# Recurrent mixers regrouped on TensorE, and masks added by one fp32r product for all heads of a bank

## The chip, the cores and the metric

The kernel runs on one core of one Trainium2 chip. The metric is device time in microseconds (us) of one execution. Before the change the median of three runs is 1646.14 us (1645.08 to 1652.29).

## What is computed

Two layers of a hybrid mixer over 1024 tokens of width 1024, each followed by a residual sum and a layer norm. A layer projects its input to some 4000 columns, feeds four groups of four heads of 64, and projects their outputs back:

```python
y_a = flat(banded_attention(q_a, k_a, heads(cols['a_v']), A_WINDOW, a_sinks)) * silu(cols['a_z'])
...
h_b = mlstm_chunkwise(...)
y_b = jax.nn.sigmoid(cols['b_o']) * flat(h_b) * silu(cols['b_z'])
...
o_c = hgrn2_chunkwise(heads(silu(cols['c_q'])), heads(jnp.log(f_c)), heads(1.0 - f_c), heads(cols['c_i']))
...
o_d = nsa_attention(...)
y = jnp.concatenate([y_a, y_b, y_c, y_d], axis=-1)
```

Group A is attention in a window of 128 tokens, with a sink. Group D joins three attentions: over compressed blocks, over selected blocks, and in a window of 512. Groups B and C are recurrences in chunks: a state is carried from chunk to chunk, and inside a chunk every query meets the earlier keys with a decay. In B the weight of key s for query t is

```python
D = jnp.where(causal, b[..., :, None] - b[..., None, :] + i_[..., None, :], -jnp.inf)
...
S = jnp.einsum('bhtd,bhsd->bhts', q_, k_) * jnp.exp(D - m_t[..., None])
num = jnp.einsum('bhts,bhsv->bhtv', S, v_) + w_inter[..., None] * jnp.einsum('bhtk,bhvk->bhtv', q_, C)
```

and in C the output of a chunk is the sum of the products inside it and of the queries with the state S:

```python
o = jnp.einsum('bhts,bhsv->bhtv', A, v_) + jnp.einsum('bhtk,bhkv->bhtv', q_ * jnp.exp(a), S)
S_new = jnp.exp(a_last[:, :, 0, :])[..., None] * S + jnp.einsum('bhsk,bhsv->bhkv', k_ * jnp.exp(a_last - a), v_)
```

All operands and results are float32.

## The kernel before

Tokens go in tiles of 128. A *stage* is one half (512 tokens, four tiles) of one layer, so there are four stages; each works through the groups D, C, A, B in this order. Projections and the attention scores take each float32 operand as a high and a low fp32r part and add three products (hi x hi, hi x lo, lo x hi; the weights are split by `load_piece`, L260 on, with ACT for the high and POOL for the low part). Products of plain float32 operands, such as P V and most of B and C, run as two records each in the trace; a transpose is one.

The order of work comes from two places. At the bottom of `tile_hybrid` a loop weaves groups: for each of the four tiles of the current group's mixer it issues one projection of the next group (`projections`, L1136, and the loop below it). Over that the framework's scheduler puts each engine's instructions in order when the program is built, by a simulated timeline; it also sets the semaphores. On the chip every engine then runs its own queue in that order. PSUM has one bank each per buffer: three for scores (psS), two for transposes (psT), two for projections (pj), one for outputs (psO).

The places that the change touches:

- **Constants** (L93 to L130, L221 to L245). `masks` holds three 128x128 masks of 0 and -1e30 (causal, its complement for the window's far edge, and the transposed causal one for B); `cmask` masks the compressed keys; `identb` is a bf16 identity. A mask is added to scores in PSUM by a product of the identity with the mask. `sel` is 128x512 of ones in rows 32c+h, so that four rows of it spread one row of numbers over 128 partitions. `load_consts` brings them in through buffers of tag P, with a cast on POOL (L242), in the first stage after the first projection.
- **`scores`** (L354 to L418), used by A and D. The keys are cut into at most two pieces of up to 512; a PSUM bank holds `hb` heads (four of 128 keys, two of 256, one of more). For each head there are two fp32r products (L377, and L381 or L379) and then bf16 mask products of 128 columns: L383 for the window's far edge, L385 for the diagonal. DVE then takes the maximum of the bank (L387), ACT the exponential (L392).
- **`group_D` front**, L620: the compressed mask is added for four heads by one bf16 product.
- **`group_C`**, the loop over chunks. `front(c+1)` comes first (decays on POOL, L761 to L764; products S_ab, L796 and L801, of 64x64). Then, for four heads, the state product L831 (64 rows, 64 columns, only if there is an earlier chunk) and the product with Vc L832 (128 rows, 64 columns) alternate into one bank Oc. Then the transposes kt_ps (L836), their copy kh on ACT (L838), the products of the new state s_ps (L843) and its update on DVE (L847 to L849).
- **`group_B`**, preparation (L962 to L999) once a stage: gates `lf`, transposed to rows `r_ps`, running sums and maxima `R` (rB, rU, rM, rE, each 128x128, where chunk c and head h sit in row 32c+h), and the carry `rk` by chunk. `front(c)` (L1002 on) fills two banks SW: the causal mask by a bf16 product of 256 columns (L1008), the row rM spread over 128 partitions by a plain float32 product of four rows for each head (L1012), and beside them Q K (L1017). `xb` (L1032) spreads rE in the same way, 64 partitions to a head.

Of the kernel before, what the change touches and what calls it, by code (L numbers as in the profile page):

```python
# [89 lines left out]
def consts():  # L90
# [5 lines left out]
    c['masks'] = np.stack([lo, up, lo.T], 1).astype(np.float32)  # L96
# [29 lines left out]
    sel = np.zeros((128, 4, 128), np.float32)  # L126
    for h in range(4):
        sel[h::32, h, :] = 1.0
    c['sel'] = sel.reshape(128, 512)
# [16 lines left out]
def tile_hybrid(ctx, tc, I, out, dbg=None, depth=DEPTH):  # L146
# [3 lines left out]
    def f(ap):  # L150
        return ap.bitcast(F32)
# [69 lines left out]
    masks = const.tile([128, 3, 128], BF16, name="masks_bf")  # L221
    cmask = const.tile([128, NT, 64], BF16, name="cmask_bf")
    identb = const.tile([128, 128], BF16, name="ident_bf")
# [4 lines left out]
    sel = const.tile([128, 512], F32, name="sel_sb")  # L228
# [4 lines left out]
    G.tensor_copy(identb, ident)  # L233

    def load_consts():

        for name, dst in (('masks', masks), ('cmask', cmask), ('lvm', lvm)):
            d2 = dst.rearrange("p a b -> p (a b)")
            n = d2.shape[1]
            m_ = mp.tile([128, 512], F32, tag="P", name="m_", bufs=PB)  # L240
            SY.dma_start(m_[:, :n], I[name] if name == 'lvm' else I[name].rearrange("p a b -> p (a b)"))
            G.tensor_copy(d2, m_[:, :n])  # L242
        for name, dst in (('rowok', rowok), ('rope_e', rope_e), ('impk', impk), ('sel', sel)):
            SY.dma_start(dst, I[name])
# [109 lines left out]
    def scores(i, k0, A1, A2, kcols, Kblk, weigh, win, sink=None, A3=None):  # L354
# [10 lines left out]
        for c, (a, b) in enumerate(cuts):  # L365
            n = b - a
            hb = 4 if n <= 128 else 2 if n <= 256 else 1
            Pc = [mp.tile([128, 2, 512], F32, tag="P", name="P", bufs=PB) for _ in range(2)]
            P.append(Pc)
            for h0 in range(0, NH, hb):  # L370
                Sp = psS.tile([128, 512], F32, tag="S", name="S_ps")[:, :hb * n].rearrange("p (h k) -> p h k", h=hb)
                for z in range(hb):
                    h = h0 + z
                    o_ = Sp[:, z, :]
                    m0, m1 = lo_mask and c == 0, b == nk * 128
                    kc_ = kcols(h, a, b)
                    PE.matmul(o_, A1[:, h, :], kc_, start=True, stop=False)  # L377
                    if Kblk is not None:
                        PE.matmul(o_, A3[:, h, :], Kblk[:, a:b], start=False, stop=not (m0 or m1))  # L379
                    else:  # L380
                        PE.matmul(o_, A2[:, h, :], kc_, start=False, stop=not (m0 or m1))  # L381
                    if m0:
                        PE.matmul(o_[:, 0:128], identb, masks[:, 1, :], start=False, stop=not m1)  # L383
                    if m1:
                        PE.matmul(o_[:, n - 128:n], identb, masks[:, 0, :], start=False, stop=True)  # L385
# [54 lines left out]
    def groups(stage):  # L440
# [83 lines left out]
        def group_D():  # L524
# [86 lines left out]
            def front(t):  # L611
# [8 lines left out]
                PE.matmul(Sc3, identb, bc(cmask[:, i, :nc_], 4, 0), start=True, stop=False)  # L620
# [76 lines left out]
        def group_C():  # L697
# [121 lines left out]
            for c in range(NTH):  # L819
# [4 lines left out]
                O = psO.tile([128, 256], F32, tag="O", name="Oc")  # L824
                for ct in range(2):
                    for hh in range(2):
                        h = 2 * ct + hh
                        rows = slice(64 * hh, 64 * hh + 64)
                        o_ = O[rows, ct * 128:(ct + 1) * 128]
                        if i > 0:  # L830
                            PE.matmul(o_, St[rows, ct, :], qe[rows, ct * 128:(ct + 1) * 128], start=(ct == 0), stop=False)  # L831
                        PE.matmul(o_, Vc[:, c, 64 * h:64 * h + 64], Af[:, hh, ct, :], start=(i == 0 and ct == 0), stop=(ct == 1))  # L832
                if i < NT - 1:
# [4 lines left out]
                    S.copy(out=kh.rearrange("p a b -> p (a b)"), in_=kt_ps)  # L838
                    s_ps = psT.tile([128, 2, 64], F32, tag="T", name="s_ps")
# [73 lines left out]
        def group_B():  # L913
# [55 lines left out]
            V.tensor_tensor(lf[:, 0, :].rearrange("p (c w) -> p c w", c=4)[:, :, 0:4], l1, l0, op=OP.subtract)  # L969
            V.tensor_copy(lf[:, 1, :].rearrange("p (c w) -> p c w", c=4)[:, :, 0:4], gi[:, :, 12:16])  # L970
# [5 lines left out]
            rk = sm.tile([128, 4], F32, tag="rk", name="rk")  # L976
            V.tensor_tensor_scan(rB, ones, r_ps[:, 0, :], 0.0, op0=OP.mult, op1=OP.add)
# [4 lines left out]
            if hf == 1:  # L982
                V.tensor_copy(rk[0:4, 0:1], mcar[0:4, :])
            for c in range(NTH):
                p_ = slice(32 * c, 32 * c + 4)
                dst = rk[32 * c + 32:32 * c + 36, 0:1] if c < NTH - 1 else mcar[0:4, :]
# [4 lines left out]
            V.tensor_scalar(rE, rM, rk[:, 0:1], None, op0=OP.add)  # L991
            u_ps = psT.tile([128, 2, 128], F32, tag="T", name="u_ps")
# [9 lines left out]
            def front(c):  # L1002
                i = T0 + c
                cs_ = slice(c * 128, (c + 1) * 128)
                p_ = slice(32 * c, 32 * c + 4)
                SW = [psS.tile([128, 512], F32, tag="S", name="SW") for _ in range(2)]
                for hh in range(2):
                    PE.matmul(SW[hh][:, 0:256].rearrange("p (h t) -> p h t", h=2), identb, bc(masks[:, 2, :], 2, 0),  # L1008
                              start=True, stop=False)
                    for ct in range(2):  # L1010
                        h = 2 * ct + hh
                        PE.matmul(SW[hh][:, ct * 128:(ct + 1) * 128], sel[p_, h * 128:(h + 1) * 128], rM[p_, :],  # L1012
                                  start=False, stop=(ct == 1))
# [17 lines left out]
                for p in range(2):  # L1031
# [178 lines left out]
```

## Time and profile before

| | |
|---|---|
| runs, median (range) | 1646.14 us (1645.08 to 1652.29) |
| the profiled execution, its own time | 1654.33 us |
| its span | 1652.5 us |
| mean granted TensorE clock | 0.962 |
| chain that ended last, TensorE and DVE | 66% and 19% |
| moved by DMA | 126.70 MB, mean 77 GB/s |

The span is the time from the first to the last recorded instruction; the execution's own time has a little around it. PE is TensorE's matmuls, PEld its weight loads, DVE VectorE, ACT ScalarE, POOL GpSimd, SP the queue that issues DMAs. A row of the timeline gives the start and the duration in us, the engine, the line, the operation, the tile written and the tiles read, for a matmul rows*columns of the array and the shape that is streamed, and how many records are merged (x4). Durations of matmuls overlap, because they are pipelined: the time that one occupies TensorE is the distance to the next start. A row of a source line or a tile gives the shortest, median and longest duration in ns. Brackets name idle time before an instruction, and who ended it.

### The profile page before, as it was taken

What the parts mean: (1) busy time and instruction counts of PE and PEld (TensorE: products, weight loads), DVE (VectorE), ACT (ScalarE), POOL (GpSimd) and SP (SyncE); (2) the same over time, 40 slices, a digit from 0 to 9 for tenths busy, and PEclk for the clock granted to TensorE, in tenths of its full rate; (3) what the DMA queues carried; (4) which work ended last, traced back from release to release, by engine and by line L of the source; (5) the groups of instructions that cost most, each with busy time, mean ns of one, the idle gap of its engine ahead of it and who ended that gap; (6) DMA issues with size and microseconds to landing.
All of it is one profiled execution on the core that took longest, in us unless ns stands there. A gap on an engine that the chain in (4) does not pass through costs nothing.

```text
span 1652.5 us, 29596 instructions
## 1 busy us (share of the span) xinstructions
PE 1538.6 (93%) x10948; PEld 1206.1 (73%) x10948; DVE 1026.2 (62%) x2454; ACT 798.3 (48%) x1865; POOL 848.7 (51%) x1173
## 2 busy tenths in 40 slices
PE   4999999899979989999998999999997999999995
PEld 3787688678767657787877768786886765688774
DVE  6256835874787776357447676456448777735737
ACT  2356535544356664455435653444434666434541
POOL 4733784546643138634575468544565321873442
PEclk9999999989989999999999999999998999799997
DMA  5322023441441001224134212233134210022311
GB/s 180 91 64 59 15 76 90 155 142 45 120 144 52 26 1 46 65 68 142 44 108 153 74 33 56 55 107 105 36 105 160 55 52 1 20 66 65 90 52 51
DMA packets 64752, 126.70 MB, mean 77 GB/s; under 512 B 10112, under 2 KB 16032, under 8 KB 64608
## 3 DMA queue, kind: packets, MB, share of 16 engines
q1 hardware_dynamic: 63744, 122.72, 25.4%
q8 instruction: 86, 1.41, 0.4%
q10 hardware_dynamic: 864, 2.10, 0.3%
q14 instruction: 58, 0.48, 0.1%
HBM read 114.30 MB, written 10.49 MB: 76 GB/s over the span
## 4 chain that ended last, share of the span: by engine, by line
PE 66%; DVE 19%; POOL 5%; issue 3%; DMA 3%; ACT 3%; SPq 0%; DVEq 0%; POOLq 0%; ACTq 0%
PE ps_f L307 7%; PE ps_f L306 6%; PE ps_f L305 6%; PE ps_p L290 5%; PE ps_p L291 4%; PE ps_p L292 4%; PE ps_pt L427 4%; PE O L434 4%; PE ps_o L478 2%; PE ps_o L476 2%; PE S_ps L377 2%; DVE QK L950 2%; PE ps_o L477 2%; PE S_ab L796 2%; DMA w_raw<-in_w_in 2%
## 5 line engine op out<-in xcount | busy, mean ns | idle before, releaser
L267 POOL TENSOR_TENSOR w_split<-w_raw,w_split 128x512 fp32r<-128x512 f32 (+2 forms) x320 | 416.0, 1307 | 380.7 <-ACT w_split L266 350.6
L266 ACT CAST w_split<-w_raw 128x512 fp32r<-128x512 f32 (+2 forms) x320 | 194.4, 611 | 238.9 <-DMA w_raw<-in_w_in 109.5
L305 PE MATMUL ps_f<-hT_hi,w_split 128*128 128x512 f32 x608 | 246.0, 405 | 0.0
L306 PE MATMUL ps_f<-hT_lo,w_split 128*128 128x512 f32 x608 | 244.0, 401 | 0.0
L307 PE MATMUL ps_f<-hT_hi,w_split 128*128 128x512 f32 x608 | 243.5, 402 | 0.0
L290 PE MATMUL ps_p<-w_split,hT_hi 128*128 128x256 f32 (+1 forms) x768 | 227.3, 298 | 8.0 <-DVE hT_lo L257 5.5
L291 PE MATMUL ps_p<-w_split,hT_hi 128*128 128x256 f32 (+1 forms) x768 | 222.8, 291 | 0.0
L292 PE MATMUL ps_p<-w_split,hT_lo 128*128 128x256 f32 (+1 forms) x768 | 222.1, 290 | 0.0
L392 ACT ACTIVATE P<-S_ps,stt 128x256 f32<-128x256 f32 (+3 forms) x256 | 133.8, 530 | 91.7 <-DVE stt L387 49.7
L290 PEld LDWEIGHTS ps_p<-w_split,hT_hi 128*128 128x128 f32 x768 | 149.4, 195 | 14.1 <-DVE hT_lo L257 7.2
L291 PEld LDWEIGHTS ps_p<-w_split,hT_hi 128*128 128x128 f32 x768 | 149.6, 195 | 2.2 <-issue 1.2
L292 PEld LDWEIGHTS ps_p<-w_split,hT_lo 128*128 128x128 f32 x768 | 149.2, 194 | 1.8 <-issue 1.2
L307 PEld LDWEIGHTS ps_f<-hT_hi,w_split 128*128 128x128 f32 x608 | 115.4, 190 | 28.1 <-issue 2.8
L306 PEld LDWEIGHTS ps_f<-hT_lo,w_split 128*128 128x128 f32 x608 | 115.3, 190 | 26.3 <-issue 3.3
L305 PEld LDWEIGHTS ps_f<-hT_hi,w_split 128*128 128x128 f32 x608 | 115.5, 190 | 25.6 <-issue 1.9
L387 DVE TENSOR_REDUCE stt<-S_ps 128x1 f32<-128x384 f32 (+3 forms) x182 | 111.1, 625 | 28.4 <-PE S_ps L385 15.1
L476 PE MATMUL ps_o<-w_split,Y 128*128 128x512 f32 x256 | 114.7, 448 | 8.6 <-DVE acc L483 6.7
L427 PE MATMUL ps_pt<-ident_sb,P 128*128 128x128 f32 x648 | 103.3, 286 | 8.6 <-DVE P L417 8.6
L478 PE MATMUL ps_o<-w_split,Y 128*128 128x512 f32 x256 | 106.7, 425 | 1.5 <-POOL Y L462 1.3
L427 PEld LDWEIGHTS ps_pt<-ident_sb,P 128*128 128x128 f32 x648 | 71.3, 143 | 48.6 <-issue 41.3
L477 PE MATMUL ps_o<-w_split,Y 128*128 128x512 f32 x256 | 106.0, 414 | 0.0
L434 PE MATMUL O<-PT,Vd 128*64 128x256 f32 x528 | 86.8, 413 | 7.2 <-DVE PT L432 7.0
(351 smaller groups left out, 3258.5 us busy)
## 6 DMA issues: line engine op xcount, KB each, us to landing
w_raw<-in_w_in SPq DMA_DIRECT2D x224, 256.0 KB, 2.7
w_raw<-in_w_out SPq DMA_DIRECT2D x64, 256.0 KB, 2.6
w_raw<-in_w_in SPq DMA_DIRECT2D x16, 276.0 KB, 2.8
w<-in_w SPq DMA_DIRECT2D x8, 512.0 KB, 4.4
hs<-acc SPq DMA_DIRECT2D x8, 512.0 KB, 2.6
h_t<-hs SPq DMA_DIRECT2D x8, 512.0 KB, 4.4
acc<-hs SPq DMA_DIRECT2D x8, 512.0 KB, 4.2
out<-acc SPq DMA_DIRECT2D x7, 512.0 KB, 2.6
```

The costliest lines, as they stand in the source:

```text
L266: S.copy(out=hi, in_=raw_)
L267: G.tensor_tensor(lo, raw_, f(hi), op=OP.subtract)
L290: PE.matmul(ps[:, :n], a, hi, start=(k == 0), stop=False)
L291: PE.matmul(ps[:, :n], a, lo, start=False, stop=False)
L292: PE.matmul(ps[:, :n], b, hi, start=False, stop=(k == 7))
L305: PE.matmul(ps, a, x1, start=(k == 0), stop=False)
L306: PE.matmul(ps, a, x2, start=False, stop=False)
L307: PE.matmul(ps, b, x1, start=False, stop=(k == 7))
L427: PE.transpose(ps[:, h, :], P[c][h // 2][:, h % 2, kb * 128 - a:kb * 128 - a + 128], ident)
L434: PE.matmul(O[64 * g:64 * g + 64, :], Vt(k0 + kb, g), PT[:, 2 * g:2 * g + 2, :].rearrange("p a b -> p (a b)"), start=(first and kb == 0), ...
L476: PE.matmul(ps, a, hi, start=(k == 0), stop=False)
L478: PE.matmul(ps, b, hi, start=False, stop=(k == 1))
```

## The change

- Masks, compressed masks and the identity become fp32r. In `scores` only the first product of a bank starts it, and the masks follow after all heads of the bank, as one product that reads the mask once for each head (stride 0): 128 columns for each head, or, where both masks meet in a piece of 256 keys, both as 256 columns for each head. The masks' order in the constant is changed so that these two are neighbours.
- In C the transposes kt_ps and the copy kh come ahead of Oc, and all four state products come ahead of all four products with Vc.
- In B `lf` holds each head twice (columns 0 and 8 of a chunk's 32), so the rows R do too. Ten new DVE operations a stage split rM and rE into a high part (fp32r) and a low rest, put the one into the first copy's rows and the other into the second's, and spread them to `RB`, six blocks of 128 columns in which only the rows of one head (rM) or of a pair of heads (rE) are not zero. `sel` grows to 128x1024 and is fp32r. One fp32r product of 128 rows and 256 columns then spreads rM for two heads, and one spreads rE for both pairs. The mask product of B is fp32r.
- One subtraction and the copies of the other gate into `lf` are made twice, the copies on POOL instead of DVE. `load_consts` takes `sel` through a P buffer and a cast on POOL, and loads a small new constant `rowsel`.

```diff
-    c['masks'] = np.stack([lo, up, lo.T], 1).astype(np.float32)
+    c['masks'] = np.stack([up, lo, lo.T], 1).astype(np.float32)
...
+    sel = np.zeros((128, 2, 4, 128), np.float32)
     for h in range(4):
-        sel[h::32, h, :] = 1.0
-    c['sel'] = sel.reshape(128, 512)
+        for k in range(4):
+            for row in (32 * k + h, 32 * k + 8 + h):
+                sel[row, 0, k, :] = 1.0
+                sel[row, 1, k, 64 * (h % 2):64 * (h % 2) + 64] = 1.0
+    c['sel'] = sel.reshape(128, 1024)
...
-        for name, dst in (('masks', masks), ('cmask', cmask), ('lvm', lvm)):
+        for name, dst in (('masks', masks), ('cmask', cmask), ('lvm', lvm), ('sel', sel)):
...
             G.tensor_copy(d2, m_[:, :n])
...
-                    PE.matmul(o_, A1[:, h, :], kc_, start=True, stop=False)
+                    PE.matmul(o_, A1[:, h, :], kc_, start=(z == 0), stop=False)
...
+                if m0 and m1 and n == 256:
+                    PE.matmul(Sp, identr, bc(masks[:, 0:2, :].rearrange("p a b -> p (a b)"), hb, 0), start=False, stop=True)
+                else:
                     if m0:
-                        PE.matmul(o_[:, 0:128], identb, masks[:, 1, :], start=False, stop=not m1)
+                        PE.matmul(Sp[:, :, 0:128], identr, bc(masks[:, 0, :], hb, 0), start=False, stop=not m1)
                     if m1:
-                        PE.matmul(o_[:, n - 128:n], identb, masks[:, 0, :], start=False, stop=True)
+                        PE.matmul(Sp[:, :, n - 128:n], identr, bc(masks[:, 1, :], hb, 0), start=False, stop=True)
...
-                PE.matmul(Sc3, identb, bc(cmask[:, i, :nc_], 4, 0), start=True, stop=False)
+                PE.matmul(Sc3, identr, bc(cmask[:, i, :nc_], 4, 0), start=True, stop=False)
...
-                O = psO.tile([128, 256], F32, tag="O", name="Oc")
-                for ct in range(2):
-                    for hh in range(2):
-                        h = 2 * ct + hh
-                        rows = slice(64 * hh, 64 * hh + 64)
-                        o_ = O[rows, ct * 128:(ct + 1) * 128]
-                        if i > 0:
-                            PE.matmul(o_, St[rows, ct, :], qe[rows, ct * 128:(ct + 1) * 128], start=(ct == 0), stop=False)
-                        PE.matmul(o_, Vc[:, c, 64 * h:64 * h + 64], Af[:, hh, ct, :], start=(i == 0 and ct == 0), stop=(ct == 1))
                 if i < NT - 1:
                     kt_ps = psT.tile([128, 256], F32, tag="T", name="kt_ps")
...
+                O = psO.tile([128, 256], F32, tag="O", name="Oc")
+                if i > 0:
+                    for ct in range(2):
+                        for hh in range(2):
+                            rows = slice(64 * hh, 64 * hh + 64)
+                            PE.matmul(O[rows, ct * 128:(ct + 1) * 128], St[rows, ct, :], qe[rows, ct * 128:(ct + 1) * 128],
+                                      start=(ct == 0), stop=False)
+                for ct in range(2):
+                    for hh in range(2):
+                        h = 2 * ct + hh
+                        PE.matmul(O[64 * hh:64 * hh + 64, ct * 128:(ct + 1) * 128], Vc[:, c, 64 * h:64 * h + 64], Af[:, hh, ct, :],
+                                  start=(i == 0 and ct == 0), stop=(ct == 1))
...
+            RB = mp.tile([128, 6, 128], F32R, tag="RB", name="RB")
+            for src, j, n, tmp in ((rM, 0, 4, rk2[:, 0]), (rE, 4, 2, rk2[:, 1])):
+                V.tensor_copy(RH, src)
+                V.tensor_tensor(tmp, src, f(RH), op=OP.subtract)
+                V.tensor_scalar(tmp, tmp, rowsel[:, 1:2], None, op0=OP.mult)
+                V.scalar_tensor_tensor(tmp, f(RH), rowsel[:, 0:1], tmp, op0=OP.mult, op1=OP.add)
+                V.tensor_tensor(RB[:, j:j + n, :], bc(tmp, n, 0), rowsel[:, 2 + j:2 + j + n].unsqueeze(2).to_broadcast([128, n, 128]),
+                                op=OP.mult)
...
-                    PE.matmul(SW[hh][:, 0:256].rearrange("p (h t) -> p h t", h=2), identb, bc(masks[:, 2, :], 2, 0),
+                    PE.matmul(SW[hh][:, 0:256].rearrange("p (h t) -> p h t", h=2), identr, bc(masks[:, 2, :], 2, 0),
                               start=True, stop=False)
-                    for ct in range(2):
-                        h = 2 * ct + hh
-                        PE.matmul(SW[hh][:, ct * 128:(ct + 1) * 128], sel[p_, h * 128:(h + 1) * 128], rM[p_, :],
-                                  start=False, stop=(ct == 1))
+                    PE.matmul(SW[hh][:, 0:256].rearrange("p (h t) -> p h t", h=2), sel[:, c * 128:(c + 1) * 128],
+                              RB[:, hh:4:2, :], start=False, stop=True)
...
-                for p in range(2):
-                    PE.matmul(xb[:, p, :], sel[p_, 256 * p + 64:256 * p + 192], rE[p_, :], start=True, stop=True)
+                PE.matmul(xb, sel[:, 512 + c * 128:512 + (c + 1) * 128], RB[:, 4:6, :], start=True, stop=True)
```

## What was predicted

> **What bounds the kernel now.** I read the page first (busy shares, the slices, the shares of the chain that ended last), then windows over the recurrent mixers, then the timeline of TensorE inside a chunk of each.
>
> ```profile
> span 1652.5 us, 29596 instructions
> PE 1538.6 (93%) x10948; PEld 1206.1 (73%) x10948; DVE 1026.2 (62%) x2454; ACT 798.3 (48%) x1865; POOL 848.7 (51%) x1173
> PE   4999999899979989999998999999997999999995
> PE 66%; DVE 19%; POOL 5%; issue 3%; DMA 3%; ACT 3%; SPq 0%; DVEq 0%; POOLq 0%; ACTq 0%
> ```
>
> TensorE is busy in nine tenths or more of nearly every slice, and two thirds of the chain lie on it: projections of the next group are woven into each mixer, so TensorE seldom lacks work. What matters is therefore how many microseconds of TensorE the change frees, and whether another engine lets them count. The windows of the first C mixer, the first B and the last B (columns: PE, PEld, DVE, ACT, POOL busy, clock, DMA):
>
> ```profile
> 178.00:263.00 85.00, 81.53 (x918) 64.74 (x918) 45.11 (x131) 33.75 (x68) 68.21 (x119) 0.96 0.19 52
> 330.00:425.00 95.00, 91.74 (x605) 75.71 (x604) 51.29 (x123) 38.20 (x81) 53.75 (x73) 0.95 0.31 95
> ...
> 1558.00:1652.00 94.00, 74.52 (x367) 57.17 (x365) 54.70 (x135) 30.70 (x69) 34.07 (x35) 0.85 0.17 51
> ```
>
> In C TensorE idles 3.5 of 85 us, but POOL is busy for 68. In B nothing else is near TensorE. In the last B, where no group follows, TensorE idles 19.5 of 94.
>
> **The change part by part.** Matmuls overlap, so I price them from start to the next start, never by the duration column.
>
> *Group C.* One chunk in the middle of C:
>
> ```profile
> 219.43 0.38 PE L831 MATMUL Oc<-qe,St 64*64 64x128 f32 x2
> 219.74 0.43 PE L832 MATMUL Oc<-Af,Vc 128*64 128x128 f32 x2
> ...
> 222.27 0.39 PE L290 MATMUL ps_p<-w_split,hT_hi 128*128 128x256 f32 x1
> ```
>
> Eight pairs alternate between two shapes, 0.36 us each, 2.84 us in all. The change puts the four state products together and then the four Af products; neighbours of one shape then use different halves of the array. Rows that do this already:
>
> ```profile
> 1577.59 0.71 PE L1017 MATMUL SW<-QK 64*128 64x128 f32 x8
> 1578.24 0.37 PE L1032 MATMUL xb<-R,sel_sb 4*128 4x128 f32 x1
> ...
> 179.72 0.65 PE L434 MATMUL O<-PT,Vd 128*64 128x256 f32 x4
> 180.30 0.66 PE L427 MATMUL ps_pt<-ident_sb,P 128*128 128x128 f32 x4
> ```
>
> Eight records of 64 rows and 128 columns take 0.65 us to the next shape; four of 128x64 with 256 columns, as many columns as eight with 128, take 0.58. So a chunk costs 0.65+0.58 = 1.23 and saves 1.61; in the 14 chunks that have a state (16 less the first of each layer) **22.5 us** of TensorE. Bounds: 0 if the instructions end up interleaved as before, 2.84 x 14 = 40 at the far end; I take the rows of the same shapes. The transposes of kt, moved ahead, are the same two, and the copy to kh now lies beside the O products; I count nothing for it (bounds: it costs its 0.2 us a chunk, or saves the wait of s_ps, as much).
>
> *Group B, front.* One chunk:
>
> ```profile
> 383.01 0.28 PE L290 MATMUL ps_p<-w_split,hT_hi 128*128 128x256 f32 x1
> 383.13 0.28 PE L291 MATMUL ps_p<-w_split,hT_hi 128*128 128x256 f32 x1
> ...
> 383.37 0.28 PE L1008 MATMUL SW<-masks_bf,ident_bf 128*128 128x256 bf16 x1
> 383.58 0.71 PE L1012 MATMUL SW<-R,sel_sb 4*128 4x128 f32 x4
> 384.22 0.48 PE L1017 MATMUL SW<-QK 64*128 64x128 f32 x2
> 384.63 0.71 PE L1032 MATMUL xb<-R,sel_sb 4*128 4x128 f32 x4
> 385.27 0.71 PE L1063 MATMUL ND<-Cs,qw 128*128 128x130 f32 x4
> ```
>
> A chunk has two banks of mask (0.21) and row products (0.64), and xb (0.64): 2.34 us. Afterwards it has five fp32r products of 256 columns with full 128 rows: 0.12 each as L290 and L291 show, and I add 0.1 twice for the change of shape against L1017 (the mask before a new shape took 0.21 instead of about 0.12). That is 0.8, saving 1.54, in 16 chunks **24.6 us**. Bounds: all five at 0.21 give 20.6; no change of shape gives 27.8.
>
> *Masks in A and D.* One head of A, and the narrow products of D:
>
> ```profile
> 1500.57 0.37 PE L377 MATMUL S_ps<-KA,A 128*128 128x256 f32 x1
> 1500.77 0.28 PE L381 MATMUL S_ps<-KA,A 128*128 128x256 f32 x1
> 1500.89 0.23 PE L383 MATMUL S_ps<-masks_bf,ident_bf 128*128 128x128 bf16 x1
> 1500.96 0.22 PE L385 MATMUL S_ps<-masks_bf,ident_bf 128*128 128x128 bf16 x1
> 1500.99 0.48 PE L476 MATMUL ps_o<-w_split,Y 128*128 128x512 f32 x1
> ...
> 504.41 0.28 PE L622 MATMUL Sc<-Kc,A 128*128 128x64 f32 x1
> 504.52 0.28 PE L623 MATMUL Sc<-Kc,A 128*128 128x64 f32 x1
> ...
> 504.86 0.42 PE L381 MATMUL S_ps<-KD,A 128*128 128x384 f32 x1
> ...
> 505.16 0.42 PE L381 MATMUL S_ps<-KD,A 128*128 128x384 f32 x1
> ...
> 1572.12 0.40 PE L306 MATMUL ps_f<-hT_lo,w_split 128*128 128x512 f32 x1
> 1572.35 0.40 PE L307 MATMUL ps_f<-hT_hi,w_split 128*128 128x512 f32 x1
> ```
>
> A head costs 0.42, a bank of two 0.84. Afterwards: four score products at 0.12 and one mask of 512 columns at 0.23 (L306 to L307), 0.71, saving 0.13; A has 28 such banks: 3.6 us. Banks of two heads with one mask (28 in D): without L383 a head is 0.35, a bank 0.70; afterwards five times 0.12, saving 0.10: 2.8 us. Banks with one wide head (88 masks): a 384-column product with its bf16 mask took 0.30, of which 0.17 is the product (three quarters of 0.23), so the mask costs 0.13; a narrow fp32r product costs 0.11 (L622 to L623). I count 0 (bounds: 88 x 0.13 = 11 saved if it hides wholly, 88 x 0.21 = 18 lost if it takes a shape change's time as L1008 does). The six banks of four narrow heads: 0. The 16 compressed masks Sc become dearer by 0.08 at most: -1.3. Together **5.1 us**.
>
> The Trainium skill speaks against this part: "TensorE: Matmul & The Clock Gate", section "Weight-path perf modes — Fast Weight Load (FWL) and DoubleRow", says that a weight load goes faster if the type is not FP32. This trace agrees on the load itself: the bf16 identity loads in a median 96 ns, the fp32 operand in 190.
>
> ```profile
> L385 PEld LDWEIGHTS <-ident_bf x192: 95/96/146, 88.8 to 1547.5; 128*128 128x128 bf16 x192
> L377 PEld LDWEIGHTS S_ps<-KA,A x64: 186/190/201, 265.9 to 1547.1; 128*128 128x128 f32 x64
> ```
>
> By that rule the 150 masks left in A and D (28+28+88+6) would each lose 94 ns, 14 us in all. But 0.12 us from one 256-column product to the next, each with such a load, is less than the load's own 0.19: loads run under the products. I leave the 14 us out.
>
> *New DVE work in B's preparation.* Five operations on the row sums before SW (copy, subtract, scale, combine, spread) and five before xb, in four stages. Nearest rows, four operations of one size, and TensorE's wait:
>
> ```profile
> L988 DVE TENSOR_SCALAR R<-R,rk x4: 278/641/1180, 344.1 to 1570.7; 128x128 f32<-128x128 f32 x4
> L989 DVE SCALAR_TENSOR_TENSOR R<-R x4: 293/1292/1378, 347.7 to 1571.4; 128x128 f32<-128x128 f32 x4
> L990 DVE TENSOR_SCALAR R<-R x4: 215/218/2258, 349.1 to 1573.2; 128x128 f32<-128x128 f32 x4
> L991 DVE TENSOR_SCALAR R<-R,rk x4: 286/286/1209, 351.4 to 1573.5; 128x128 f32<-128x128 f32 x4
> ...
> 351.39 1.15 PE L1012 MATMUL SW<-R,sel_sb 4*128 4x128 f32 x8 [1.85 <-DVE R L990]
> ```
>
> The medians average 0.61 us, so five are 3 us. In the first stage TensorE already waits 1.85 us there with nothing else: all 3 count. In the three others it was inside projections until SW; half counts: **-7.5 us**. Bounds: 0, and ten at 2.26 in four stages, 90 us. Behind these on DVE stand the additions that empty out_proj's banks. The second subtraction into lf and the copies moved to POOL, 16 columns each, are no dearer than these rows; I count 0 for them (bounds 0 to 2 us in all).
>
> *Start.* POOL casts sel as well, 1024 columns, and the DMA ahead of it, on SP between the weight pieces, has twice the bytes:
>
> ```profile
> L242 POOL CAST cmask_bf<-m__409 x1: 1610/1610/1610, 18.0 to 18.0; 128x512 bf16<-128x512 f32 x1
> ```
>
> That is 3.2 us of POOL at 20 us, where split weights wait for it; I take **-1** (0 to -3.2, and a microsecond for the DMA).
>
> *The sum.* TensorE frees 22.5+24.6+5.1 = 52 us. I let 60% of C's count, because POOL has to be busy 68 us of a stage that would last 79 (13.5); 80% of B's in three stages (18.5 to 14.8) and 60% in the last (6.1 to 3.7); 70% in A and D (3.6). That is 35.6, less 8.5: **27 us**. The profiled execution took 1654.3 us for its span of 1652.5; 1627 follows for it, and the runs' median of 1646.1 lies 8 lower, so the forecast is **1619 us**.
>
> **The rivals.**
> 1. *Everything freed counts* and the few added operations hide: 52 less 1 to 52 with nothing lost: 1594 to 1606. For it: the slices of nine tenths, and half-clock stretches beside the four-row products (0.85 in the last B), which may shrink. Against: POOL in C. 0.17.
> 2. *POOL becomes C's bound* and the stage doesn't shorten, and half of B's counts: 12.3+3.6-8.5 = 7 us, 1639 (1632 to 1645). For it: the 68 busy us. Against: TensorE idles only 3.5. 0.16.
> 3. *The order of issue undoes the regrouping* in C (other products slip between, so the shapes still alternate): 27-13.5 = 13.5, 1633. For it: the 64-row products of L1017 already appear cut into twos above. 0.08.
> 4. *Slower: B's preparation on DVE.* If all ten operations stand in the way in each stage, the gain of 35.6-1 is gone from 0.87 us an operation; at L989's 1.29 the loss is 52 us and the time 1663; at 2.26 it is 90, 1702. SW and all matmuls behind it on TensorE wait, since each engine runs in order. For it: L989 and L990 of the first stage. Against: the mean of 0.61. 0.08.
>
> On rival 4 the Trainium skill, "SBUF — State Buffer", section "Who interferes with whom", says that a DVE operation with two SBUF inputs, or in a two-port mode, blocks against POOL for the whole instruction. The trace fits it: L990 took 0.215 and 2.258 us with one shape. By it, the two-input half of the ten would be the slow ones.
>
> **How the numbers follow.** The forecast has 0.51, its own range 1606 to 1632. Half a per cent, 8 us, is what a measurement can tell. Faster than 1638: forecast, rivals 1 and 3, and 0.06 of rival 2: 0.82. Within: 0.10 of rival 2 and 0.01 of rival 4, 0.11. Slower: 0.07. The range of 1594 to 1643 leaves out rival 4, a little of rival 2 and the far bounds of the prices, under 2 in 10.
>
> **What would show it.** In C, L831's and L832's successors as runs of eight, 1.2 us together; in B, five products 0.12 apart; A's bank 0.71; TensorE busy near 1490 us; SW waiting for the spread rows by 3 us more. Wrong would be: TensorE's idle time growing by more than half of what is freed, alternating shapes in C, or RB operations over 0.9 us.

## The result and the profile after

The changed kernel takes 1594.61 us (median of 4 runs, 1589.67 to 1595.70) against 1645.61 us before (4 runs, 1644.28 to 1652.29): a ratio of 0.9676, with an interval of 0.9643 to 0.9709, and 51 us gained where 27 were forecast. The direction and most mechanisms were right; the size was not, and 1594.61 lies below the forecast's own range (1606 to 1632), at the low end of the first rival. The page after the change, lines as before:

```profile
span 1593.9 us, 29097 instructions
PE 1471.4 (92%) x10674; PEld 1184.5 (74%) x10674; DVE 1054.0 (66%) x2494; ACT 791.5 (50%) x1865; POOL 854.2 (54%) x1182
PE   3899999989979998999998999999997999899995
PE 56%; DVE 17%; POOL 13%; DMA 5%; issue 5%; ACT 3%; SPq 0%; DVEq 0%; POOLq 0%; ACTq 0%
```

TensorE's busy time fell by 1538.6 - 1471.4 = 67.2 us and the span by 58.6, so TensorE's idle time grew by only 8.6 us (113.9 to 122.5). It is still the bound; POOL's share of the last chain rose from 5% to 13%.

The regrouped C in a middle chunk, the timeline of TensorE after (start, duration, records merged):

```profile
225.45 0.32 PE L851 MATMUL Oc<-qe,St 64*64 64x128 f32 x1
225.50 0.22 PE L816 MATMUL S_ab<-E 64*64 64x64 f32 x1
225.56 0.60 PE L851 MATMUL Oc<-qe,St 64*64 64x128 f32 x7
226.09 0.66 PE L856 MATMUL Oc<-Af,Vc 128*64 128x128 f32 x8
226.68 0.39 PE L300 MATMUL ps_p<-w_split,hT_hi 128*128 128x256 f32 x1
```

Two runs of eight, 226.68 - 225.45 = 1.23 us from the first to what follows, the forecast to the hundredth, even with one record of S_ab between. A middle chunk of B and a bank of A, in the same view:

```profile
365.51 0.28 PE L1039 MATMUL SW<-masks_r,ident_r 128*128 128x256 f32 x1
365.63 0.28 PE L1041 MATMUL SW<-RB,sel_sb 128*128 128x256 f32 x1
365.84 0.71 PE L1046 MATMUL SW<-QK 64*128 64x128 f32 x4
...
1452.44 0.28 PE L388 MATMUL S_ps<-KA,A 128*128 128x256 f32 x1
1452.56 0.28 PE L392 MATMUL S_ps<-KA,A 128*128 128x256 f32 x1
1452.68 0.28 PE L388 MATMUL S_ps<-KA,A 128*128 128x256 f32 x1
1452.80 0.28 PE L392 MATMUL S_ps<-KA,A 128*128 128x256 f32 x1
1452.91 0.40 PE L395 MATMUL S_ps<-masks_r,ident_r 128*128 128x512 f32 x1
1453.15 0.39 PE L491 MATMUL ps_o<-w_split,Y 128*128 128x512 f32 x1
```

In B the mask takes 0.12 us and the rows of two heads 0.21, with the change of shape; A's bank takes 0.71, as forecast. What the tiles occupy of TensorE in the two profiled executions (each record from its start to the next start, or its own duration where that is shorter, added up) went like this: Oc 43.0 to 17.9 us (25.1 freed, forecast 22.5), SW with xb 52.0 to 32.4 (19.6, forecast 24.6), S_ps with Sc 132.9 to 127.6 (5.3, forecast 5.1). That is 50 of the 67; the other 17 left tiles that nobody had touched (ps_o 7.3 us, ps_f 5.2, S_ab 2.4 and smaller ones). The same instructions occupied less there, and a higher clock would do that. The cores' view gives it, before and after:

```profile
core 0: 1652.5 us, clock 0.962
```

```profile
core 0: 1593.9 us, clock 0.973
```

In these traces the clock is either full or half: in windows of 2 us over the last B before, it reads 1.00 up to 1606 us, 0.50 from 1608 to 1618 and 1.00 again from 1620. So a mean of 0.962 is half clock for some 2 x 0.038 x 1652.5 = 126 us, and 0.973 for 2 x 0.027 x 1593.9 = 86; the stretches themselves add up to 125 and 87. Half of what TensorE is busy in them is lost work. It was busy for 104 of the 125 us and 70 of the 87, so (104 - 70) / 2 = 17 us of the 67 came without one product less, as much as left the untouched tiles.

The recurrent stages as sums of windows (length, then busy time of each engine; in each stage from the first to the last S_ab for C, from the first SW to the last ND for B; of the single windows the last C and the last B, with the clock third from the end), before:

```profile
1412.13:1480.72 68.59, 67.24 (x821) 54.00 (x821) 35.66 (x111) 25.11 (x50) 58.66 (x107) 0.90 0.19 48
sum 263.80, PE 254.71 PEld 206.15 DVE 149.11 ACT 95.95 POOL 229.48; mean PE 63.68 PEld 51.54 DVE 37.28 ACT 23.99 POOL 57.37
...
1554.63:1630.15 75.52, 72.23 (x372) 56.09 (x372) 41.08 (x105) 29.66 (x66) 27.93 (x32) 0.91 0.16 43
sum 361.40, PE 343.86 PEld 279.65 DVE 187.94 ACT 155.29 POOL 184.03; mean PE 85.97 PEld 69.91 DVE 46.98 ACT 38.82 POOL 46.01
```

and after:

```profile
1369.94:1431.16 61.22, 56.81 (x819) 47.82 (x819) 36.93 (x110) 22.80 (x46) 54.25 (x102) 1.00 0.19 49
sum 244.17, PE 229.67 PEld 192.75 DVE 151.71 ACT 90.88 POOL 217.05; mean PE 57.42 PEld 48.19 DVE 37.93 ACT 22.72 POOL 54.26
...
1503.10:1576.48 73.38, 66.00 (x340) 51.66 (x339) 53.06 (x123) 31.40 (x69) 34.72 (x37) 0.93 0.18 51
sum 342.41, PE 319.82 PEld 263.00 DVE 215.11 ACT 154.51 POOL 196.78; mean PE 79.95 PEld 65.75 DVE 53.78 ACT 38.63 POOL 49.19
```

C lost 19.6 us of length for 25.0 of TensorE, B 19.0 for 24.0: close to 80% of what TensorE lost there. Part of both is the clock: half clock fell from 32 to 11 us in C's windows and from 34 to 20 in B's, so up to 10 of the 19.6 and up to 7 of the 19.0. The four-row products run in B's windows alone, so this pair by itself doesn't tie the clock to them. The remaining 20 us went in D, A, the projections and the last tail.

Runs of one kernel differ mainly by the clock: over 25 runs beside the first experiments the kernel before took from 1630.97 us at 0.978 to 1653.64 at 0.966. A straight line through all 58 runs of it beside the experiments gives 1.2 us for 0.001 of clock. If TensorE were busy throughout, it would be 0.001 x 1650 = 1.65. The mean clock of the runs therefore stands beside the times below. Each ratio is to runs of the kernel before on the same chip; the chips differ from group to group, so kernels of two groups are better compared by their ratios than by their medians.

### The profile page after: what moved, and what is told of

Read it like the earlier page. It is cut to its first block, busy times and chain, and to the rows that moved or that the text cites. A ratio compares the mean times of both kernels' runs of the same rounds, so it can differ in the third digit from the quotient of the medians.

```text
span 1593.9 us, 29097 instructions
## 1 busy us (share of the span) xinstructions
PE 1471.4 (92%) x10674; PEld 1184.5 (74%) x10674; DVE 1054.0 (66%) x2494; ACT 791.5 (50%) x1865; POOL 854.2 (54%) x1182
## 4 chain that ended last, share of the span: by engine, by line
PE 56%; DVE 17%; POOL 13%; DMA 5%; issue 5%; ACT 3%; SPq 0%; DVEq 0%; POOLq 0%; ACTq 0%
PE ps_f L315 6%; PE ps_f L317 6%; PE ps_f L316 6%; PE ps_pt L442 4%; PE O L449 4%; PE ps_p L300 3%; DMA w_raw<-in_w_in 3%; PE ps_p L301 3%; PE ps_p L302 3%; POOL w_split L277 3%; PE S_ps L388 2%; PE ps_o L491 2%; PE ps_o L493 2%; DVE QK L970 2%; PE ps_o L492 2%
## 5 line engine op out<-in xcount | busy, mean ns | idle before, releaser
L316 PEld LDWEIGHTS ps_f<-hT_lo,w_split 128*128 128x128 f32 x608 | 114.9, 189 | 23.9 <-issue 0.8
L491 PE MATMUL ps_o<-w_split,Y 128*128 128x512 f32 x256 | 111.3, 435 | 10.7 <-DVE acc L498 6.5
L493 PE MATMUL ps_o<-w_split,Y 128*128 128x512 f32 x256 | 104.6, 417 | 4.3 <-POOL Y L477 4.1
L492 PE MATMUL ps_o<-w_split,Y 128*128 128x512 f32 x256 | 103.7, 405 | 0.0
```

The costliest lines, as they stand in the source:

```text
L316: PE.matmul(ps, a, x2, start=False, stop=False)
L491: PE.matmul(ps, a, hi, start=(k == 0), stop=False)
L493: PE.matmul(ps, b, hi, start=False, stop=(k == 1))
```

## The experiments

The theory to test first: B's regrouping is worth more than its freed starts, because its four-row products hold the clock down. The rivals: all the freed TensorE time of C, B and the masks simply counted; or the costs that were taken off (ten DVE operations, the start) were not there.

### Each part alone, and each part undone

| kernel | median us (runs) | ratio to before [95%] | mean clock |
|---|---|---|---|
| before, beside the four that follow | 1645.02 (25) | | 0.969 |
| before + C | 1634.04 (10) | 0.9935 [0.9906, 0.9964] | 0.965 |
| before + B's rows | 1625.89 (4) | 0.9877 [0.9837, 0.9916] | 0.974 |
| before + masks | 1640.83 (10) | 0.9999 [0.9967, 1.0031] | 0.961 |
| before + kt_ps and kh moved only | 1640.49 (10) | 0.9967 [0.9938, 0.9995] | 0.972 |
| changed | 1594.61 (4) | 0.9676 [0.9643, 0.9709] | 0.973 |
| changed, C as before | 1609.47 (4) | 0.9774 [0.9737, 0.9811] | 0.976 |
| changed, B's rows as before | 1622.58 (4) | 0.9855 [0.9820, 0.9889] | 0.961 |
| changed, masks as before | 1606.47 (4) | 0.9762 [0.9725, 0.9798] | 0.974 |

**C alone, and C undone.** The kernel before gets the two separate loops over Oc, and the changed kernel the alternating one:

```diff
-                        if i > 0:
-                            PE.matmul(o_, St[rows, ct, :], qe[rows, ct * 128:(ct + 1) * 128], start=(ct == 0), stop=False)
-                        PE.matmul(o_, Vc[:, c, 64 * h:64 * h + 64], Af[:, hh, ct, :], start=(i == 0 and ct == 0), stop=(ct == 1))
...
+                if i > 0:
+                    for ct in range(2):
+                        for hh in range(2):
...
+                            PE.matmul(O[rows, ct * 128:(ct + 1) * 128], St[rows, ct, :], qe[rows, ct * 128:(ct + 1) * 128],
...
+                for ct in range(2):
+                    for hh in range(2):
...
+                        PE.matmul(O[64 * hh:64 * hh + 64, ct * 128:(ct + 1) * 128], Vc[:, c, 64 * h:64 * h + 64], Af[:, hh, ct, :],
...
```

> Only the regrouping of C, on the kernel before. The theory that freed TensorE time counts nearly whole: Oc costs about 25 us less of TensorE, and the time falls by 20 to 28, to 1618-1626. The theory that POOL bounds C's stages: the time falls by at most 13, to 1632 or more, and TensorE's idle time grows by the rest.

> The changed kernel with C as before (kt behind, products alternating). Alone, C's regrouping brought 11 us (1645.0 to 1634.0) for 24 us of TensorE. If POOL bounds C whatever the rest does: 1594 + 11 = 1603 to 1608. If C's freed time counts whole once the other parts are in: 1616-1622.

Alone it gave 11 us, undone it took 15 (16 by the ratios); Oc occupied 23.9 us less and 23.0 more. Around the forecast of 13.5 on both sides. The clock was 0.004 lower alone and 0.003 higher undone, so at equal clock both would be some 4 to 5 us more. By the first of the two texts that speaks for POOL; the additions on POOL further down decide against it.

**The move of kt_ps and kh alone**, with the products still alternating:

```diff
+                if i < NT - 1:
+                    kt_ps = psT.tile([128, 256], F32, tag="T", name="kt_ps")
+                    ...
+                    S.copy(out=kh.rearrange("p a b -> p (a b)"), in_=kt_ps)
                 O = psO.tile([128, 256], F32, tag="O", name="Oc")
```

> Only kt's transposes and the copy kh ahead of the O products, which alternate as before. If the regrouping itself is the cause: 1642-1648, and Oc's TensorE time as before (43 us). If the earlier state, or merely another order found by the scheduler, gave the gain: 1635 or less.

4.5 us, an interval that just misses 1, at a clock 0.003 above that of before (some 4 us by 1.2 for 0.001). The move itself isn't told from nothing; the regrouping is what frees Oc's time.

**B's rows alone, and undone**:

```diff
-                        PE.matmul(SW[hh][:, ct * 128:(ct + 1) * 128], sel[p_, h * 128:(h + 1) * 128], rM[p_, :], ...
+                    PE.matmul(SW[hh][:, 0:256]..., sel[:, c * 128:(c + 1) * 128], RB[:, hh:4:2, :], ...
```

> Only B's new row products (with sel and its load at the start), masks elsewhere in bf16 as before. SW and xb cost about 18 us less of TensorE. If nothing but that counts, and the start loses the 7 us that the changed kernel loses: 1632-1638. If the half-clock stretches beside the four-row products shrink too, the granted clock rises by 0.005 to 0.01 and the time is 1618-1630. If the rows' DVE work takes the gain: 1645 or more.

> The changed kernel with B's rows as before (four-row products, small sel). Alone, B brought 19 us. If the parts add: 1594 + 19 = 1613, and the granted clock falls to about 0.963. If B's share grows beside the others: 1620-1630. If the start's 7 us come from sel's load, D's mixer begins 7 us sooner than in the changed kernel.

Alone 19 us, undone 28 (20 and 29 by the ratios), where 10 were forecast (18.5 - 7.5 - 1). Undone, the clock falls from 0.973 to 0.961. Here lies most of the error.

**The masks alone** (all of them, B's included) **and undone**:

```diff
-                        PE.matmul(o_[:, n - 128:n], identb, masks[:, 0, :], start=False, stop=True)
+                        PE.matmul(Sp[:, :, n - 128:n], identr, bc(masks[:, 1, :], hb, 0), start=False, stop=True)
```

> Only the masks in fp32r, one product for a bank (B's mask product too), rows and C as before. Theory of freed time: TensorE 5 us less in S_ps and Sc, time 1639-1643. If the longer weight loads of the fp32r identity count: 150 x 0.094 = 14 us more, 1655-1660.

> The changed kernel with bf16 masks for each head in A and D (and B's mask in bf16). Alone the masks brought 4 us at a clock lower by 0.008, about 11 at the same clock. If the masks count only by their 5 us of TensorE: 1598-1602. If they bring more beside the others (the scores' maxima start sooner): 1603-1610. If the fp32r masks lower the clock, the clock here is higher than 0.973.

Alone a ratio of 0.9999, though S_ps was 5.7 us lighter; the clock, 0.961, was among the two lowest. Undone 12 us (14 by the ratios), where S_ps became 6.9 us heavier. With intervals of some 5 us alone and 8 undone this is 3.6 as forecast or three times as much.

The parts alone add up to 34 us, undone to 55 (31 and 60 by the ratios), and the whole gave 51.

### Full rows without gathering

The kernel before, with the same number of row products of the same width and type; only, each contracts over all 128 rows, with a `sel` of 128x2048 in which the other rows are zero:

```diff
-        sel[h::32, h, :] = 1.0
-    c['sel'] = sel.reshape(128, 512)
+            sel[32 * k + h, k, h, :] = 1.0
+    c['sel'] = sel.reshape(128, 2048)
...
-                        PE.matmul(..., sel[p_, h * 128:(h + 1) * 128], rM[p_, :],
+                        PE.matmul(..., sel[:, 512 * c + h * 128:512 * c + (h + 1) * 128], rM,
```

> The kernel before with the spreading products of B still in plain float32 and one for each head, but over all 128 rows (sel is zero in the rows of other chunks and heads, 128x2048). As many records as before. If four-row products make the clock fall to half: the granted clock rises from 0.969 to 0.974 or more, and the time falls by 5 to 10 us less the start's cost of the larger sel (DMA only, 1 MB). If it is TensorE's change of shape that costs, SW and xb get cheaper by up to 0.1 us at each of the changes (3 in a chunk, 5 us). If neither: 1645-1655.

1629.57 us (10 runs) against 1648.66 (13), ratio 0.9892 [0.9867, 0.9917], with nothing gathered: 18 us, about twice what was expected. SW and xb occupied 8.4 us less; some 4 of these are records that ran at half clock before (29 of 352, 8.0 us in all), and some 4 are at full clock, where a row product now took 0.126 us from start to start instead of 0.152. That fits the rival of the text, the change of shape, as the smaller part of the 18. The mean clock of the ten runs was 0.977 (0.974 to 0.978), of before 0.968. Over 1630 us, 0.009 are 2 x 0.009 x 1630 = 29 us at half clock, at most 15 us of work, and 11 by 1.2 us for 0.001. The row products (duration shortest, median, longest in ns) in the view of SW, and B's last window, both of this kernel:

```profile
L1012 PE MATMUL SW<-R,sel_sb x128: 271/275/377, 352.7 to 1587.9; 128*128 128x128 f32 x128
```

```profile
1536.15:1604.57 68.42, 64.56 (x373) 51.54 (x372) 41.26 (x104) 29.80 (x66) 27.70 (x33) 1.00 0.17 47
```

and the row products before:

```profile
L1012 PE MATMUL SW<-R,sel_sb x128: 269/270/577, 351.4 to 1609.7; 4*128 4x128 f32 x128
```

The medians are the same, 0.27 us. The longest is 0.577 with four rows, which is a product at half clock, and 0.377 with 128; the clock in B's last window went from 0.91 to 1.00. One trace alone would prove little: the changed kernel still has 0.93 there. But over all profiled kernels B's windows differ in this way. In B's four windows together half clock lasted 14 to 58 us in the six with sliced rows, 14 to 20 in the eight with gathered rows, and 7 and 10 in the two with one full product for each head. In C's windows it scatters from 1 to 32 us.

### Rows of 32

Is it the few filled rows, or that the product uses a slice of the array? The kernel before with slices of 32 rows, the other 28 times zero:

```diff
-                p_ = slice(32 * c, 32 * c + 4)
+                p_ = slice(32 * c, 32 * c + 32)
```

> The kernel before, but each row product of B contracts over a slice of 32 rows (the four it needs, the other 28 multiplied by zeros) in place of 4; the number of products, their order, type and width stay. If the few filled rows hold the granted clock down, most of what the 128 rows gained comes back: 1630 to 1637 us, mean clock 0.974 or more, SW 4 to 7 us of TensorE below before. If it is the form of the product (a slice of the array in place of the whole of it, and the change between the two), nothing changes: 1645 +-5 us, clock about 0.968, half-clock time inside B's mixers as before.

1643.95 us (10 runs), ratio 0.9983 [0.9959, 1.0007], clock 0.970 against 0.968: as before. The same two rows for this kernel:

```profile
L1012 PE MATMUL SW<-R,sel_sb x128: 270/270/518, 352.1 to 1604.6; 32*128 32x128 f32 x128
```

```profile
1551.01:1624.19 73.18, 69.22 (x372) 53.66 (x372) 41.64 (x105) 29.78 (x66) 28.11 (x32) 0.95 0.16 44
```

Eight times the rows did nothing. What brings the clock up lies between 32 rows in a slice and 128 rows in the whole array; whether it is the number of rows or the missing change between slice and whole, these runs don't separate.

### The changed kernel with full rows in place of the gathered ones

C and the masks as changed, B's rows one plain product per head over 128 rows; RB and its ten operations are gone, and `sel` (128x2048) is loaded at the first B.

```diff
-                    PE.matmul(SW[hh][:, 0:256]..., sel[:, c * 128:(c + 1) * 128], RB[:, hh:4:2, :], start=False, stop=True)
+                    for ct in range(2):
+                        h = 2 * ct + hh
+                        PE.matmul(SW[hh][:, ct * 128:(ct + 1) * 128], sel[:, 512 * c + h * 128:512 * c + (h + 1) * 128], rM, ...
```

> The changed kernel with C regrouped and the masks in fp32r, but B's rows as one plain fp32 product per head over all 128 rows, without RB and its ten VectorE operations per stage. Against the changed kernel SW and xb cost TensorE about 11 us more, the RB chain's 5 us go, the half-clock time inside B's mixers goes (about 8 us of loss at most). If B's gain is mostly the clock: 1586 to 1596 us, as fast as the changed kernel or faster. If it is mostly the four products gathered in one: 1600 to 1608 us.

1599.81 us (4 runs), ratio 0.9724 [0.9677, 0.9771], clock 0.974. Against the same kernel with four rows (1622.58, clock 0.961) that is 23 us (22 by the ratios) for filling the rows alone; SW and xb account for 8.9 of them on TensorE, and 0.013 of clock for 0.013 x 1620 = 21 at most, 16 by 1.2 us for 0.001. The gathered form of the change is another 5 us below it (1594.61; 8 by the ratios), with intervals that meet: its 13 us less on TensorE (SW 9.5, xb 3.7) are paid in part with the ten operations. So three quarters to four fifths of B's 28 us would have come from full rows alone. The bounds set beforehand said otherwise: 1599.81 stands at the edge of the range for gathering, because they allowed 8 us for the clock. No variant beat the changed kernel by more than its interval.

### What was taken off

**The ten operations twice**:

```diff
-            for src, j, n, tmp in ((rM, 0, 4, rk2[:, 0]), (rE, 4, 2, rk2[:, 1])):
...
+            for _ in range(2):
+                for src, j, n, tmp in ((rM, 0, 4, rk2[:, 0]), (rE, 4, 2, rk2[:, 1])):
...
```

> The changed kernel with the ten DVE operations that build RB done twice in each stage (the second time over the first, same numbers). By the prediction's term, 7.5 us for one set, it is 6 to 9 us slower: 1601-1604. If TensorE has projections to do meanwhile and the set costs nearly nothing: within 3 us of the changed kernel. If DVE's queue behind them matters: more than 12 us slower.

1599.95 us (4 runs), ratio 0.9727 [0.9677, 0.9778]: some 5 us by the medians and 8 by the ratios for ten more, with intervals that meet, near the 7.5 taken off. B's windows add up to 349.75 us instead of 342.41, 7.3 more. In the changed kernel the first five take little each (the timeline of DVE in the first B):

```profile
353.57 0.21 DVE L1018 CAST RH<-R 128x128 fp32r<-128x128 f32 x1
...
353.82 0.29 DVE L1019 TENSOR_TENSOR rk<-R,RH 128x128 f32<-128x128 f32 x1
...
354.85 0.69 DVE L1022 TENSOR_TENSOR RB<-rk,rowsel_sb 128x512 fp32r<-128x512 f32 x1
```

From 353.57 to the end of L1022, 355.54, it is 2.0 us for five, where 3 were taken, and TensorE waits for that:

```profile
355.60 0.50 PE L1041 MATMUL SW<-RB,sel_sb 128*128 128x256 f32 x2 [1.97 <-DVE RB L1022]
```

This wait (the timeline of TensorE after) stands where one of 1.85 us for R stood; it took its place and grew by only 0.1.

**`sel` loaded at the first B**, not at the start:

```diff
-        for name, dst in (('masks', masks), ('cmask', cmask), ('lvm', lvm), ('sel', sel)):
+        for name, dst in (('masks', masks), ('cmask', cmask), ('lvm', lvm)):
...
+            if stage == 0:
+                m_ = mp.tile([128, 1024], F32, tag="P", name="m_", bufs=PB)
+                SY.dma_start(m_, I['sel'])
+                G.tensor_copy(sel, m_)
```

> The changed kernel, with sel (512 KB, its P buffer and POOL cast) loaded at the beginning of B's first projections instead of in the first 25 us. If the 7 us lost before D's first mixer come from that load: 1586-1590, with TensorE's first score products of D 5 to 7 us earlier. If they come from another order of the work: 1592-1597.

1591.75 us (4 runs), ratio 0.9675 [0.9644, 0.9706]: not told from the changed kernel. The first scores of D (the view of S_ps: durations, then first and last start) in the kernel before, the changed one and this one:

```profile
L377 PE MATMUL S_ps<-KD,A x192: 274/364/668, 87.7 to 1400.7; 128*128 128x384 f32 x80, 128*128 128x256 f32 x56, 128*128 128x512 f32 x40, 128*128 128x128 f32 x16
```

```profile
L388 PE MATMUL S_ps<-KD,A x192: 272/338/687, 94.6 to 1357.6; 128*128 128x384 f32 x80, 128*128 128x256 f32 x56, 128*128 128x512 f32 x40, 128*128 128x128 f32 x16
```

```profile
L388 PE MATMUL S_ps<-KD,A x192: 272/338/689, 90.3 to 1354.5; 128*128 128x384 f32 x80, 128*128 128x256 f32 x56, 128*128 128x512 f32 x40, 128*128 128x128 f32 x16
```

They start at 87.7, 94.6 and 90.3 us, so the load costs the start 4 us of 7, and the end 3 by the medians, but nothing by the ratios. The cast itself took 1.04 us in the changed kernel, not 3.2 (the timeline of POOL after):

```profile
23.13 1.04 POOL L252 CAST sel_sb<-m__416 128x1024 fp32r<-128x1024 f32 x1 [0.45 <-DMA m__416<-in_sel]
```

### The rivals

**POOL in C.** The changed kernel with two more additions of 128x256 on POOL in each chunk of C, whose result nobody reads:

```diff
+                for _ in range(2):
+                    idle_ = sm.tile([128, 4, 64], F32, tag="rp1", name="rp1")
+                    G.tensor_tensor(idle_.rearrange("p a b -> p (a b)"), a2, a2, op=OP.add)
```

> The changed kernel with two more POOL additions of 128x256 in each chunk of C, ahead of the exponentials, whose results nobody reads: 32 x 0.73 = 23 us of POOL. If POOL bounds C's stages: 15 us slower or more, 1608-1618. If TensorE bounds them and POOL has slack of 12 us a stage: at most 5 us slower.

1600.15 us (4 runs), ratio 0.9724 [0.9677, 0.9771]. POOL was busy 19.5 us more by the page (873.7 against 854.2), and 5.5 came through by the medians, 8 by the ratios. C's windows add up to 244.98 us, against 244.17 without the additions, so POOL's work doesn't bound C; where the rest was lost is not traced.

**bf16 masks where a bank holds one head**:

```diff
+                if hb == 1:
+                    if m0:
+                        PE.matmul(Sp[:, 0, 0:128], identb, masksb[:, 0, :], start=False, stop=not m1)
+                    if m1:
+                        PE.matmul(Sp[:, 0, n - 128:n], identb, masksb[:, 1, :], start=False, stop=True)
+                elif m0 and m1 and n == 256:
```

> The changed kernel with bf16 masks where a bank holds one wide head (88 masks), the rest as changed. Prediction: the narrow fp32r mask costs as much as the bf16 one: within 3 us of the changed kernel, and S_ps within 2 us of TensorE. If the load of the fp32r identity is not hidden there: up to 8 us faster. If the grouping of all masks is what frees the waits on the scores: slower by 3 to 6.

1593.75 us (4 runs), ratio 0.9680 [0.9631, 0.9729], S_ps 0.5 us heavier: no difference. The 88 narrow masks were priced at 0, and cost 0.

## Why the prediction was right and wrong

- **Prices on TensorE.** C's 22.5 us measured 23 to 25, the masks' 5.1 measured 5.3, A's bank 0.71 as told. B's 24.6 was too much: 19.6. By source lines a chunk's masks, rows and xb occupied 2.20 us before on average, half clock included, where the one chunk read had 2.34, and 0.96 after where 0.80 was taken; xb alone is 0.25 for each of 16 products where 0.12 was taken.
- **C: 60% count.** The size was right within the spread: 13.5 forecast, 11 alone and 15 undone. At nearly full clock in all four stages, the full-row kernel before and the full-row kernel with C regrouped differ in C's windows by 256.09 - 242.57 = 13.5 us of length. The reason was not: the share was taken because POOL had to be busy, and more POOL work left C's windows as long as they were, so the figure is in part luck. What the trace does show is that TensorE's waits for POOL in C's four windows went from 1.3 to 6.7 us, as much as its idle time there grew. They are for single late results (the low part of Y and the rotated keys kr), not for C's decays, except 0.5 us.
- **B: the step that failed.** "80% of B's in three stages ... and 60% in the last", less 7.5 and the start, gave 10; the runs gave 19 and 28. Two things were wrong there. The sum had no term for the clock: the four-row products cost the clock as well as their starts. Full rows without any gathering are worth 18 us in the kernel before and 22 to 23 in the changed one, at a clock higher by 0.009 and 0.013, which is 11 and 16 us by 1.2 for 0.001. The prediction had quoted the rows (0.95 in the first B, 0.85 in the last) and put them under rival 1 as stretches that "may shrink", with no price; had all of that gone, it would be (1 - 0.95) x 95 + (1 - 0.85) x 94 = 19 us at most. And too much was taken off: TensorE's idle time in B's windows was to grow by 6.1 for the shares and 7.5 for the operations, and grew by 5.0 (17.5 to 22.6). The price of the set itself was not far off, as the doubling shows; but the first set took the place of a wait that was there already (1.97 us for 1.85), and the wait of 3 us more that was forecast did not come.
- **A and D.** 70% of 5.1 in the sum: 3.6. Alone nothing was resolved, undone it was 12. Whether the masks gain more than their TensorE time stays open; no run here separates it from the clock.
- **The account of the profiled pair.** This is the same step for the whole kernel. The forecast freed 52 us and gave 25 back (16.6 by the shares, 8.5 by costs). Measured were 67.2 freed, 17 of it by clock and 50 by shape, and 8.6 back as idle time. 27 + 17 of clock - 2 of shape + 16.6 less idle time is 58.6, the difference of the spans. By the runs' means the clock rose less than in this pair (0.968 or 0.969 to 0.973, 5 to 8 us), as the profiled execution before lay 8 us above its median. So the clock explains a quarter to a third of the 24 us missed; the larger rest is idle time that did not come, and why it did not is shown in part only. By the windows idle time grew by 5.4 in C (9.0 forecast) and 5.0 in B (13.6), and fell by 1.9 elsewhere, where it was to grow by 2.5.
- **The rivals.** The first was right in its time (1594 to 1606) and in naming the clock, but not in its reason that all counts: C counted in part. POOL as C's bound fell with the two additions, the undone regrouping with the timeline of C, and the slow DVE operations with the times of the 40 that were profiled: 34 took 0.21 to 0.69 us each and six 1.32 to 1.67, the sign that the prediction had named (over 0.9), but all 40 together took 20 us of DVE and B's idle time grew by 5.0. Of the six three are the cast, which reads one input, so the operations with two inputs were not the slow ones as such. Whether the six are the stall that the Trainium skill gives as a rule in "SBUF — State Buffer", section "Who interferes with whom", is not shown, and no run here shows it at a price that matters.
- **The weight load of the masks.** The 14 us that the Trainium skill's section on Fast Weight Load suggested ("TensorE: Matmul & The Clock Gate") were left out rightly: bf16 and fp32r for the 88 narrow masks gave the same time within the interval.

## What to carry to other kernels

Where the page's clock lies below 1, read it by window and price it as a term of its own: 2 x (1 - clock) of the length is half clock, and half of what TensorE is busy in it is lost work. A product of few rows was no shorter here than a full one (0.27 us both), and the clock was lower: padding four rows to 128 with zeros, at the same count, gave 18 of 1648 us and is a cheaper first try than gathering. Group products by shape where two shapes alternate: eight pairs fell from 2.84 to 1.23 us with no instruction less.

## What was not expected of the hardware

- With the same number of row products, the mean clock was 0.968 with 4 rows, 0.970 with 32 and 0.977 with 128. The Trainium skill, "TensorE: Matmul & The Clock Gate", section "Part 1: The HAM clock gate", has the clock follow how busy TensorE has been lately, at half or full rate. Both rates are seen here; but in B's last window the kernel before was busy for 72.23 of 75.52 us at a clock of 0.91, and the one with 128 rows for 64.56 of 68.42, no larger a share, at 1.00. Busy time alone doesn't tell which of them throttles; what does is not shown here.
- All kernels that keep the sliced row products had mean clocks of 0.961 to 0.972, all with full rows 0.970 to 0.977, so the two ranges touch. The two lowest, 0.961, are the masks alone and the change without B's rows, that is, less TensorE work beside the same slices. No run takes this further.
- A 128x1024 cast to fp32r took POOL 1.04 us, where a 128x512 cast to bf16 had taken 1.61.
